# The first mixers' products added to h by VectorE from PSUM, in place of a staging tile and a GpSimd addition

## The chip, the core and the metric

The kernel runs on one core of a Trainium2 chip. The metric is the device time of one execution, in microseconds. The engines are named as the profile names them: PE is TensorE (matmuls), PEld its weight loads, DVE is VectorE, ACT is ScalarE, POOL is GpSimd, SP is SyncE, which issues the DMAs. SBUF is the on-chip memory, PSUM the accumulation memory that TensorE writes.

## The reference

One layer of a streaming encoder on 1024 frames of 1024 features, in float32:

```python
h = x
hn = rms_norm(h, norm_mix_g[i])
z_a, z_b, z_c, z_d = _split(hn @ w_in[i], [A_COLS, B_COLS, C_COLS, D_COLS])
o_a = gmlp_spatial_gating(z_a, ...)     # mixer 0
o_b = gated_deltanet(z_b, ...)          # mixer 1
o_c = rwkv7_time_mix(z_c, ...)          # mixer 2
o_d = conformer_conv(z_d, ...)          # mixer 3
h = h + jnp.concatenate([o_a, o_b, o_c, o_d], axis=-1) @ w_out[i]
hn = rms_norm(h, norm_ffn_g[i])
gate = causal_depthwise_conv(hn @ w_ffn_gate[i], ffn_conv_w[i])
h = h + (jax.nn.silu(gate) * (hn @ w_ffn_up[i])) @ w_ffn_down[i]
hn = rms_norm(h, norm_ple_g[i])
h = h + (p[i] @ w_ple_proj[i]) * jax.nn.sigmoid(hn @ w_ple_gate[i])
return rms_norm(h, final_norm_g)
```

Each mixer owns 256 of the 1024 columns. The line that matters here is the projection with `w_out`: it is a sum over the four mixers, so the kernel adds each mixer's part to h when that mixer's output is there.

## The kernel before

The frames are 8 tiles of 128 rows. Every matmul operand is split into a high part and a low part of a narrower type, and a product is three matmuls (`mm3`, L136): high by high, high by low, low by high.

The kernel has a first phase (input projection and the mixers' elementwise parts), a second phase (the recurrence of mixer 2, tile by tile), and then the feed-forward part and the last gate. At the end of the first phase VectorE inverts the lower triangular 32x32 blocks of mixer 2: `invert` is a chain of 31 steps, each with multiplications (L216) and subtractions (L220) on small SBUF operands, where each step needs the one before. In front of it a transposition makes its input (L1043, tile `rCs`), behind it two transpositions (L1147, L1149) give the tiles `rTc` and `Tn`, from which TensorE builds larger blocks (L1158, L1160). The tiles' recurrence can only start then.

`wout_early` gives TensorE work for that time: the parts of mixers 3 and 0, and then that of mixer 1. For each tile it loads the mixers' outputs (`oaf`), splits them (high part `osph` on ScalarE, L109; low part `ospl` on VectorE, L112) and multiplies them with the split weights (`wh`, `wl`), a half of 512 columns at a time: for mixers 3 and 0 a half is 12 matmuls into one of two PSUM buffers (the tag `psh`). In the first pass (`staged`, 8 tiles, 16 halves) ScalarE copies each half into the staging tile `stg` (L423), and GpSimd adds the tile to h (L425). In the other passes VectorE adds each half to h straight from PSUM (L427). The weights of mixers 1 and 2 are loaded and split (`wh` on ScalarE, `wl` on VectorE or GpSimd) into the buffers that the weights of mixers 3 and 0 leave. The staging tile shares its one buffer with `xn`, the normalised rows of a tile in `fnorm`.

A scheduler orders the instructions of each engine from their dependencies and priorities: the program's order is the priority, `tc.cur_priority` shifts whole parts back (`wout_early` by 100,000 and, for mixer 1, more), and `self.top()` puts what is made in it ahead of all else that is ready. An engine runs its instructions in the order so fixed, and each waits for the semaphores of what it needs.

Of the kernel before, what the change touches and what calls it, by code (L numbers as in the profile page):

```python
# [9 lines left out]
F32 = mybir.dt.float32  # L10
# [3 lines left out]
ALU = mybir.AluOpType  # L14
# [3 lines left out]
P = 128  # L18
S = 1024
D = 1024  # L20
# [77 lines left out]
class Net:  # L98
# [309 lines left out]
    def wout_tile(self, t, ofs, ws, staged=False, tag="osp", k="h"):  # L408

        nc = self.nc  # L410
        with self.top():
            os = [self.split(of, tag, [P, 2, P], 3 if tag == "osp" else 2, self.wo if tag == "osp" else self.p2) for of in ofs]
        for half in range(2):
            cs = slice(half * 512, half * 512 + 512)
            ps = self.mps(k)
            n = 2 * len(ofs)
            for j in range(n):
                (oh, ol), w = os[j // 2], ws[j // 2][j % 2]
                self.mm3(ps, oh[:, j % 2, :], ol[:, j % 2, :], w[0][:, cs], w[1][:, cs], j == 0, j == n - 1)
            if staged:  # L420
                if half == 0:
                    stg = self.wo.tile([P, D], F32, name="stg", tag="nxn", bufs=1)
                nc.scalar.copy(out=stg[:, cs], in_=ps)  # L423
                if half == 1:
                    nc.gpsimd.tensor_tensor(out=self.h[:, t, :], in0=stg, in1=self.h[:, t, :], op=ALU.add)  # L425
            else:
                nc.vector.tensor_tensor(out=self.h[:, t, cs], in0=ps, in1=self.h[:, t, cs], op=ALU.add)  # L427
            yield

# [1226 lines left out]
```

## Time and profile before

| | before |
|---|---|
| median of 3 runs | 1472.71 us (1472.57 to 1479.37) |
| the profiled execution | 1470.72 us |
| its span | 1468.9 us |
| TensorE busy | 1383.5 us (94%) |
| VectorE busy | 1038.8 us (71%) |
| ScalarE busy | 602.9 us (41%) |
| GpSimd busy | 467.2 us (32%) |
| mean granted clock of TensorE | 0.972 of 2.4 GHz |

A share of busy time is a mean over stages with different limits. A time in a row of the trace counts from the span's start. The time in brackets behind a row is what the engine stood idle before it, and behind the arrow is what ended that idle time.

### The profile page before, as it was taken

To read this page: it belongs to the slowest core of one execution; us is meant where nothing else is said; L and a number is where in the kernel's file an instruction comes from. 1 tells how busy PE (TensorE), PEld (TensorE's weight loads), DVE (VectorE), ACT (ScalarE), POOL (GpSimd) and SP (SyncE) were. 2 spreads that over 40 slices of the span, in tenths; PEclk is the share of its full clock that TensorE was granted. 3 is DMA by queue.
4 is the path that set the end of the run, shared out by engine and by line. 5 is a ranking of instruction groups with operands and counts; after the bars stand their busy time and mean duration, and the time that the engine had idled before them with its cause. 6 is when DMAs were issued, how large, how long until landed. Compare 5 with 4: busy or idle time off the path is not lost.

```text
span 1468.9 us, 21095 instructions
## 1 busy us (share of the span) xinstructions
PE 1383.5 (94%) x7864; PEld 1106.8 (75%) x7864; DVE 1038.8 (71%) x1773; ACT 602.9 (41%) x999; POOL 467.2 (32%) x432
## 2 busy tenths in 40 slices
PE   7998999799998889998799999999999999999997
PEld 6887877677766667776577888888888778877785
DVE  6599868776499677776487767776665695778543
ACT  7252363132642233336343333333333344445554
POOL 3304145262323341124421222222221454574000
PEclk9999999799999799999899999999999999999999
DMA  6111123132155333123533233322233993374132
GB/s 224 54 38 44 58 93 109 31 109 59 68 205 187 100 118 100 62 94 135 185 131 136 94 108 108 107 88 82 92 106 101 297 309 109 94 253 155 30 114 86
DMA packets 91734, 171.77 MB, mean 117 GB/s; under 512 B 12400, under 2 KB 41712, under 8 KB 91376
## 3 DMA queue, kind: packets, MB, share of 16 engines
q1 hardware_dynamic: 91344, 169.93, 34.8%
q8 instruction: 62, 1.02, 0.3%
q10 hardware_dynamic: 288, 0.49, 0.1%
q14 instruction: 40, 0.33, 0.1%
HBM read 120.85 MB, written 49.55 MB: 116 GB/s over the span
## 4 chain that ended last, share of the span: by engine, by line
PE 66%; DVE 18%; issue 5%; ACT 4%; POOL 3%; DMA 3%; SPq 0%; POOLq 0%; DVEq 0%; ACTq 0%
PE pf L136 40%; PE mps L136 13%; DVE cy L571 4%; DMA w<-in_wd 2%; DVE Xt L216 2%; DVE X L220 2%; PE mps L1082 1%; POOL wl L1227 1%; DVE wl L1227 1%; DVE w L1223 1%; PE mps L1178 1%; PE mps L879 1%; DVE by L195 1%; PE px L136 1%; PE mps L1160 1%
## 5 line engine op out<-in xcount | busy, mean ns | idle before, releaser
L136 PE MATMUL mps<-hT,wh 128*128 128x512 f32 (+1 forms) x736 | 233.8, 398 | 8.4 <-DVE by L195 3.8
L136 PEld LDWEIGHTS mps<-hT,wh 128*128 128x128 f32 x736 | 137.0, 192 | 39.7 <-issue 4.7
L136 PE MATMUL mps<-hT,wl 128*128 128x512 f32 (+1 forms) x368 | 145.5, 395 | 0.6 <-POOL wl L112 0.6
L1227 POOL TENSOR_TENSOR wl<-yr,wh 128x512 fp32r<-128x512 f32 x73 | 106.7, 1466 | 95.6 <-ACT wh L1226 82.9
L112 POOL TENSOR_TENSOR wl<-raw,wh 128x1024 fp32r<-128x1024 f32 x25 | 72.2, 2892 | 197.0 <-ACT wh L109 195.7
L136 PE MATMUL pf<-wl,wh 128*128 128x512 f32 x300 | 117.8, 392 | 3.9 <-DVE wl L1227 3.8
L136 PE MATMUL pf<-wh 128*128 128x512 f32 x300 | 117.1, 391 | 2.0 <-ACT wh L1226 2.0
L136 PE MATMUL pf<-wh,wl 128*128 128x512 f32 x300 | 117.0, 390 | 0.0
L1223 DVE TENSOR_TENSOR pf<-pf,u 128x512 f32<-128x512 f32 x88 | 61.0, 694 | 69.9 <-PE pf L136 69.8
L1226 ACT CAST fq<-s 128x512 fp32r<-128x512 f32 x88 | 53.5, 619 | 121.7 <-PE pf L136 96.5
L1227 POOL TENSOR_TENSOR fq<-raw,fq 128x512 fp32r<-128x512 f32 (+1 forms) x31 | 50.2, 1618 | 154.1 <-ACT fq L1226 154.1
L1227 DVE TENSOR_TENSOR wl<-w,wh 128x512 fp32r<-128x512 f32 x62 | 71.7, 1163 | 37.5 <-ACT wh L1226 37.2
L571 DVE SCALAR_TENSOR_TENSOR cy<-csg,prmt,cy 128x1023 f32<-128x1023 f32 (+29 forms) x60 | 83.0, 1408 | 7.1 <-ACT cy L568 6.6
L1227 POOL TENSOR_TENSOR wl<-raw,wh 128x1024 fp32r<-128x1024 f32 (+1 forms) x17 | 40.3, 2378 | 143.8 <-issue 116.6
L136 PEld LDWEIGHTS mps<-hT,wl 128*128 128x128 f32 x368 | 70.7, 192 | 16.5 <-issue 0.8
L1226 ACT CAST wh<-yr 128x512 fp32r<-128x512 f32 x73 | 45.1, 619 | 79.1 <-POOL wl L1227 49.4
L136 PEld LDWEIGHTS pf<-wl,wh 128*128 128x128 f32 x300 | 56.3, 188 | 18.1 <-DVE wl L1227 6.6
L1227 DVE TENSOR_TENSOR fq<-s,fq 128x512 fp32r<-128x512 f32 x66 | 45.5, 692 | 30.7 <-ACT fq L1226 30.7
L136 PEld LDWEIGHTS pf<-wh 128*128 128x128 f32 x300 | 56.3, 188 | 14.2 <-ACT wh L1226 2.5
L136 PE MATMUL pf<-xT2h,fq 128*128 128x512 f32 x176 | 60.4, 405 | 5.1 <-ACT fq L1226 5.1
L136 PEld LDWEIGHTS pf<-wh,wl 128*128 128x128 f32 x300 | 56.3, 188 | 11.3
L136 PE MATMUL pf<-xT4h,fq 128*128 128x512 f32 x176 | 59.1, 396 | 1.6 <-DVE pf L1223 1.6
(484 smaller groups left out, 3577.3 us busy)
## 6 DMA issues: line engine op xcount, KB each, us to landing
yr<-d_y SPq DMA_DIRECT2D x73, 256.0 KB, 3.0
w<-in_wd SPq DMA_DIRECT2D x55, 256.0 KB, 4.8
raw<-in_wg SPq DMA_DIRECT2D x24, 512.0 KB, 3.7
raw<-in_wu SPq DMA_DIRECT2D x24, 512.0 KB, 3.5
raw<-in_win SPq DMA_DIRECT2D x22, 512.0 KB, 3.7
d_y<-fy SPq DMA_DIRECT2D x11, 512.0 KB, 3.6
d_y<-ys SPq DMA_DIRECT2D x11, 512.0 KB, 3.4
d_y<-ys SPq DMA_DIRECT2D x22, 256.0 KB, 3.8
```

What stands on the lines that cost most here:

```text
L112: (eng or self.nc.vector).tensor_sub(out=lo, in0=raw, in1=hi.bitcast(F32))
L136: mm = lambda *a, **k: self.nc.tensor.matmul(*a, skip_group_check=more, **k)
L195: V.scalar_tensor_tensor(out=yh[:, j:], in0=ps[:, 0:512 - j], scalar=ws[j], in1=yh[:, j:], op0=ALU.mult, op1=ALU.add)
L216: nc.vector.tensor_tensor(out=t3[:, q], in0=A[:, j + 1 + q.start:j + 1 + q.stop, j:j + 1].broadcast_to([P, k, m]), in1=X[:, j:j + 1, 0:m]. ...
L220: nc.vector.tensor_tensor(out=X[:, rows, 0:m], in0=X[:, rows, 0:m], in1=t3[:, q], op=op)
L571: nc.vector.scalar_tensor_tensor(out=yc[:, sh:], in0=gl[:, 0:S - sh], scalar=self.prm("cfw", 2 * j + c), in1=yc[:, sh:], op0=ALU.mult, op1 ...
L879: nc.tensor.matmul(pS[:, pr * 64:pr * 64 + 64], x["E"][:, pr, c, :], S0[:, pr, :], start=True, stop=True)
L1082: nc.tensor.matmul(pa[:, pr, c], bk[rw, pr, c, :], cin[rw, 0:2, pr, cc[c]], start=True, stop=True)
L1160: nc.tensor.matmul(pq[c][r1, v], Q[r2, u], Tc[r2, u], start=True, stop=True)
L1223: eng.tensor_tensor(out=out, in0=a, in1=b, op=op)
L1226: self.nc.scalar.copy(out=hi, in_=raw)
L1227: eng.tensor_sub(out=lo, in0=raw, in1=hi.bitcast(F32))
```

## The change

In the staged pass, too, VectorE adds each half to h straight from PSUM, in the same form as in the other passes, and with the priority of `top()`. The two ScalarE copies and the GpSimd addition of each tile are gone, and with them the staging tile.

```diff
             for j in range(n):
                 (oh, ol), w = os[j // 2], ws[j // 2][j % 2]
                 self.mm3(ps, oh[:, j % 2, :], ol[:, j % 2, :], w[0][:, cs], w[1][:, cs], j == 0, j == n - 1)
-            if staged:
-                if half == 0:
-                    stg = self.wo.tile([P, D], F32, name="stg", tag="nxn", bufs=1)
-                nc.scalar.copy(out=stg[:, cs], in_=ps)
-                if half == 1:
-                    nc.gpsimd.tensor_tensor(out=self.h[:, t, :], in0=stg, in1=self.h[:, t, :], op=ALU.add)
-            else:
+            with self.top() if staged else nullcontext():
                 nc.vector.tensor_tensor(out=self.h[:, t, cs], in0=ps, in1=self.h[:, t, cs], op=ALU.add)
             yield
```

Lines behind the change have numbers that are lower by 6 in the changed kernel: L427 is L421 there, L1043 is L1037. The change also moves instructions on the engines. VectorE, in the middle of the inversion (`X` and `Xt` are its tiles, `ospl` a low part for TensorE), before:

```order
L216 TENSOR_TENSOR Xt<-rCs,X 128x108
L112 TENSOR_TENSOR ospl<-oaf,osph 128x256
L220 TENSOR_TENSOR X<-X,Xt 128x11x9
L220 TENSOR_TENSOR X<-X,Xt 128x12x9
L216 TENSOR_TENSOR Xt<-rCs,X 128x110 x2
L220 TENSOR_TENSOR X<-X,Xt 128x11x10 x2
L216 TENSOR_TENSOR Xt<-rCs,X 128x110
L216 TENSOR_TENSOR Xt<-rCs,X 128x121
L220 TENSOR_TENSOR X<-X,Xt 128x10x11
L112 TENSOR_TENSOR ospl<-oaf,osph 128x256
```

And the same place in the changed kernel:

```order
L216 TENSOR_TENSOR Xt<-rCs,X 128x108
L421 TENSOR_TENSOR h<-mps,h 128x512
L220 TENSOR_TENSOR X<-X,Xt 128x11x9
L220 TENSOR_TENSOR X<-X,Xt 128x12x9
L216 TENSOR_TENSOR Xt<-rCs,X 128x110 x2
L220 TENSOR_TENSOR X<-X,Xt 128x11x10
L112 TENSOR_TENSOR ospl<-oaf,osph 128x256
L220 TENSOR_TENSOR X<-X,Xt 128x11x10
L216 TENSOR_TENSOR Xt<-rCs,X 128x110
L216 TENSOR_TENSOR Xt<-rCs,X 128x121
L220 TENSOR_TENSOR X<-X,Xt 128x10x11
L421 TENSOR_TENSOR h<-mps,h 128x512
```

An addition stands where a low part stood, and the low part comes a few places later. Twelve of the sixteen additions stand between the transposition in front of the inversion and its last step: two in a row behind the second step, and then one about every ten rows.

GpSimd at the start of the second phase (`sbdT` is the operand built for a tile's recurrence, `rQ`, `rof` and `psp` other tiles of it and of filling work, `wl` a weight's low part), before:

```order
L1227 TENSOR_TENSOR psp<-pin,psp 128x256
L1101 TENSOR_SCALAR rQ<-rcin 128x256
L112 TENSOR_TENSOR wl<-raw,wh 128x1024
L1202 TENSOR_SCALAR sbdT_5047<-rTc 32x4x32 x4
L1204 TENSOR_SCALAR sbdT_5047<-rMo_3666 32x4x32 x2
L425 TENSOR_TENSOR h<-stg,h 128x1024
L1139 TENSOR_TENSOR rof<-rof,rcg 128x256
L1101 TENSOR_SCALAR rQ<-rcin 128x256
L112 TENSOR_TENSOR wl<-raw,wh 128x1024 x2
L1139 TENSOR_TENSOR rof<-rof,rcg 128x256 x2
```

And in the changed kernel, from the second tile's `rQ` on:

```order
L1095 TENSOR_SCALAR rQ<-rcin 128x256
L112 TENSOR_TENSOR wl<-raw,wh 128x1024
L1196 TENSOR_SCALAR sbdT_5031<-rTc 32x4x32 x4
L1198 TENSOR_SCALAR sbdT_5031<-rMo_3665 32x4x32 x2
L1095 TENSOR_SCALAR rQ<-rcin 128x256
L1221 TENSOR_TENSOR psp<-pin,psp 128x256
L112 TENSOR_TENSOR wl<-raw,wh 128x1024
L1196 TENSOR_SCALAR sbdT_5032<-rTc 32x4x32 x4
L1198 TENSOR_SCALAR sbdT_5032<-rMo_3665 32x4x32 x2
L1221 TENSOR_TENSOR psp<-pin,psp 128x256
L1095 TENSOR_SCALAR rQ<-rcin 128x256
L112 TENSOR_TENSOR wl<-raw,wh 128x1024
```

The three conversions of the weights of mixers 1 and 2 on GpSimd stand one in each of three tiles, the first two ahead of where the first stood. On ScalarE their high parts move with them. On TensorE 161 of the 192 matmuls of the staged pass stand in front of the first L1158, where 156 stood.

## Rows read from the trace of the kernel before

**Rows 1.** By stretches: us, busy us (instructions) by engine, PEclk, DMA share, GB/s.

```profile
445.00:470.00 25.00, 21.07 (x83) 16.57 (x83) 23.84 (x81) 6.63 (x15) 8.15 (x5) 0.93 0.48 165
...
485.00:505.00 20.00, 16.00 (x274) 12.75 (x275) 11.24 (x19) 4.06 (x8) 3.92 (x6) 0.50 0.17 48
570.00:600.00 30.00, 29.33 (x261) 22.74 (x260) 23.04 (x59) 11.97 (x28) 4.63 (x14) 1.00 0.21 71
```

**Rows 2.** PE in order of time: start us, us, instruction [idle before <-releaser].

```profile
456.74 0.50 PE L136 MATMUL mps<-wh,ospl 128*128 128x512 f32 x1 [3.72 <-DVE ospl L112]
...
458.12 0.63 PE L136 MATMUL mps<-wl,osph 128*128 128x512 f32 x1
458.55 0.63 PE L136 MATMUL mps<-wh,ospl 128*128 128x512 f32 x1
...
486.24 0.80 PE L136 MATMUL mps<-wh,ospl 128*128 128x512 f32 x1 [4.19 <-DVE ospl L112]
```

**Rows 3.** The staging tile's instructions: ns min/median/max, first and last start.

```profile
L423 ACT COPY stg<-mps x16: 578/586/593, 444.7 to 536.4; 128x512 f32<-128x512 f32 x16
L425 POOL TENSOR_TENSOR h<-stg,h x8: 2337/2376/2671, 446.2 to 539.8; 128x1024 f32<-128x1024 f32 x8
```

**Rows 4.** DVE in order of time, inside the inversion.

```profile
446.89 2.01 DVE L112 TENSOR_TENSOR ospl<-oaf,osph 128x256 fp32r<-128x256 f32 x1
...
451.87 2.54 DVE L216 TENSOR_TENSOR Xt<-rCs,X 128x56 f32<-128x56 f32 x2
454.33 0.33 DVE L220 TENSOR_TENSOR X<-X,Xt 128x56 f32<-128x56 f32 x2
...
456.27 0.42 DVE L112 TENSOR_TENSOR ospl<-oaf,osph 128x256 fp32r<-128x256 f32 x1
...
463.25 2.41 DVE L112 TENSOR_TENSOR ospl<-oaf,osph 128x256 fp32r<-128x256 f32 x1 [0.38 <-ACT osph L109]
...
469.38 2.41 DVE L216 TENSOR_TENSOR Xt<-rCs,X 128x126 f32<-128x126 f32 x1
...
472.04 0.28 DVE L216 TENSOR_TENSOR Xt<-rCs,X 128x126 f32<-128x126 f32 x1
...
476.10 2.47 DVE L220 TENSOR_TENSOR X<-X,Xt 128x110 f32<-128x110 f32 x1
...
483.57 2.28 DVE L216 TENSOR_TENSOR Xt<-rCs,X 128x60 f32<-128x60 f32 x1
```

**Rows 5.** POOL in order of time: two of the eight additions.

```profile
451.85 2.36 POOL L425 TENSOR_TENSOR h<-stg,h 128x1024 f32<-128x1024 f32 x1 [3.23 <-ACT stg L423]
...
539.78 2.36 POOL L425 TENSOR_TENSOR h<-stg,h 128x1024 f32<-128x1024 f32 x1
```

**Rows 6.** Groups of instructions: the addition from PSUM; busy us, mean ns | idle before.

```profile
L427 DVE TENSOR_TENSOR h<-mps,h 128x512 f32<-128x512 f32 x32 | 21.9, 687 | 7.8 <-PE mps L136 7.5
```

**Rows 7.** In order of time, 539 to 547 us: DVE, POOL and PE.

```profile
539.44 2.79 DVE L882 COPY sbdS<-rS 64x128 f32<-64x128 f32 x2
...
542.28 0.54 PE L896 MATMUL mps<-sbdS,rQ 128*64 128x128 f32 x5 [0.73 <-DVE sbdS L882]
...
544.26 0.73 PE L136 MATMUL mps<-wh,osch 128*128 128x512 f32 x2 [1.22 <-ACT wh L109]
544.29 4.78 POOL L112 TENSOR_TENSOR wl<-raw,wh 128x1024 fp32r<-128x1024 f32 x2 [0.86 <-ACT wh L109]
...
545.18 0.41 DVE L898 TENSOR_TENSOR oloc<-mps,oloc 128x256 f32<-128x256 f32 x1
...
546.66 2.50 DVE L882 COPY sbdS<-rS 64x128 f32<-64x128 f32 x2
...
546.73 0.79 PE L136 MATMUL mps<-wl,osch 128*128 128x512 f32 x1 [0.58 <-POOL wl L112]
```

**Rows 8.** L136 alone by stretches: us, PE busy (x), PEld busy (x), PEclk, DMA share, GB/s.

```profile
461.42:474.90 13.48, 13.48 (x60) 10.90 (x58) 1.00 0.64 210
485.00:505.00 20.00, 8.70 (x18) 5.48 (x19) 0.50 0.17 48
```

## The prediction

> **What bounds the kernel now.** I read the view by stretches first, then VectorE's instructions in order of time, then TensorE's, then the tile that the change removes. The changed products run while VectorE inverts the 32x32 blocks of the last mixer (L216 multiplies, L220 subtracts, each step needing the one before). In 445 to 470 us VectorE is busy 23.84 us of 25, TensorE 21.07 [rows 1]: VectorE sets the end here and TensorE waits for it, for instance 3.72 us and 4.19 us for VectorE's low part of a mixer output [rows 2]. In 485 to 505 us TensorE holds a granted clock of 0.50, the 1.2 GHz level; from 570 us it is busy 29.33 us of 30 at 1.00 [rows 1]. So time won in the inversion arrives at the end, and behind it TensorE is the bound: there its idle time counts, not VectorE's.
>
> **What is removed.** Sixteen ScalarE copies of 586 ns and eight GpSimd additions of 2,376 ns [rows 3]. ScalarE waits for TensorE in this stretch, so its copies are worth nothing by themselves. The GpSimd additions are worth much, through VectorE: while one runs, a VectorE instruction that reads SBUF takes as long as the addition does. The six that fall in the inversion have each one such row [rows 4]. Against the nearest undisturbed row of the same kind:
>
> - L112 at 446.89: 2.01 - 0.42 = 1.59 us
> - L216 at 451.87 (a pair): 2.54 - 0.33 = 2.21
> - L112 at 463.25: 2.41 - 0.42 = 1.99
> - L216 at 469.38: 2.41 - 0.28 = 2.13
> - L220 at 476.10: 2.47 - 0.28 = 2.19
> - L216 at 483.57: 2.28 - 0.28 = 2.00
>
> The GpSimd rows at 451.85 and 539.78, 2.36 us each, show the pattern [rows 5]. Sum: 12.11 us off VectorE's chain.
>
> **What is added.** Sixteen VectorE additions of 128x512 from PSUM. The kernel has 32 of that form: 687 ns each [rows 6]. The order of the changed kernel puts twelve of them between the first transposition and the end of the inversion: 12 x 0.687 = 8.24 us on the same chain. Net for the inversion: -12.11 + 8.24 = -3.87 us. The four later ones stand where VectorE is busy 11.24 us of 20 [rows 1]; I cost them at nothing, and at 4 x 0.687 = 2.7 us if that gap is gone. A GpSimd instruction beside them should not stretch them: the addition from PSUM at 545.18 took 0.41 us under a GpSimd pair that ran from 544.29 to 549.07, when the SBUF copy at 546.66 took 2.50 [rows 7].
>
> **The added wait.** Each addition waits for its half product: 12 matmuls of 512 columns. Behind it on VectorE stand the rest of the inversion and the low parts that TensorE needs next. At clock 1.00 a matmul starts every 13.48 / 58 = 0.23 us (58 weight loads in that stretch [rows 8]), so a half takes 2.8 us; at the lower clock one starts every 0.43 us (458.12 to 458.55 [rows 2]), 5.2 us a half. VectorE's pace: from 451.87 to the end of the row at 483.57 are 34.0 us [rows 4]; less the five stalls in it (10.5) and with ten additions (6.9) that is 30.4 us for ten halves, against 27.9 us that TensorE needs at full clock. Slack: 2.5 us. There are two PSUM buffers, and the first two additions come only after two steps of the inversion, some 5 us after the ScalarE copies of before (first at 444.7 [rows 3]). TensorE pauses that long. After its pause of 3.72 us the clock was at the lower level from 458.12 [rows 2] to 461.42, where a stretch at 1.00 begins [rows 8]: 3.3 / 0.43 = 8 matmuls, 0.2 us lost on each, 1.6 us. That fits into 2.5. I take 0 for the wait; the bounds are 0 and, if the clock stays low twice as long and some low parts come late, +2.4 us.
>
> The page "TensorE: Matmul & The Clock Gate" of the Trainium skill (section "A second HAM failure mode: psum-queue depth-cycling") speaks against this change: a kernel that cycles through PSUM buffers can let TensorE idle briefly so often between groups that its clock swings, and throughput is lost. What that would do here is the third rival below; the trace agrees in one place (the 8 matmuls), and not in the 13.48 us that follow at 1.00.
>
> **What moves.** The output weights of the other two mixers reuse the buffers of these two, and their conversion stands a tile earlier on GpSimd and ScalarE, as the orders show. Before, TensorE waited at 544.26 for such a weight (1.22 us), at 546.73 for its low part (0.58), and at 542.28 for a VectorE copy of 2.79 us that the GpSimd addition at 539.78 stretched (0.73) [rows 5, 7]. Those 2.53 us are TensorE's own idle time; I take all of them off. Bounds: 0 (the converted weights, 4.78 us for two on GpSimd [rows 7], stretch other VectorE rows where they stand now) and -2.53. SyncE's queue changes with this: the loads of the weights go ahead of two of mixer outputs; they wait for GpSimd's conversions, which are earlier too, so I cost that at nothing.
>
> **TensorE's low clock at 485 to 505.** It has 18 matmuls of 512 columns [rows 8], at 0.43 us instead of 0.23. The changed order has five more before the inversion ends, so the pause ahead of it is shorter. A full clock would give 18 x 0.2 = 3.6 us. A pause stays, since TensorE still has to wait for the last transposition, so I take 0; bounds 0 and -3.6.
>
> **Sum.** -3.87 - 2.53 = -6.4 us. The profiled execution took 1470.72 us, so 1464.3 on its scale; the median of the runs shown, 1472.71, lies 2.0 us above it: 1466.3 us.
>
> **Rivals.**
>
> 1. The gain is larger: the clock does not fall at 485. For it: TensorE's 4.19 us wait ahead of that stretch ends earlier, with more work before it. Against: another pause remains, and small matmuls follow. 1466.3 - 3.6 = 1462.7 us.
> 2. No change: the additions wait after all. VectorE and TensorE now hand each other a low part one way and a PSUM buffer the other, with a slack of a quarter of a microsecond per half. If each of the ten additions loses 0.4 us, the 3.87 us are gone; with the weights' gain gone too, 1472.7 us. For it: the thin slack. Against: VectorE's low parts stand right behind the additions, early enough by the same pace.
> 3. Slower: in the inversion TensorE stays at the lower clock. Ten halves then take 120 x 0.43 = 51.6 us in place of 30.4, and VectorE stands behind each: +21.2 - 3.9 = +17.3, 1490 us. It decides when more than 2.5 / 0.2 = 12 of the 120 matmuls run at the lower level; another 3.87 / 0.2 = 19 eat the inversion's gain, and with the weights' 2.53 us and the 7.4 us of the bound below it takes some 80 to be slower beyond it. Against: the trace came back to 1.00 after 8.
>
> **How the numbers follow.** Chances: forecast 0.50, first rival 0.20, second 0.22, third 0.08. A change under 0.5% (7.4 us, so 1465.3 and 1480.1) can hardly be told from none in this kernel. Faster than that: the first rival and the better part of the forecast (about two fifths of it), 0.41; slower: the third rival and a little more, 0.09; between: 0.50. Range: down 3.6 us for the clock and up to 3.7 us that the two stretched VectorE copies of 2.79 and 2.50 us [rows 7] may have held back beyond the waits listed; up 2.5 + 2.4 us for the weights and the wait, and 2.7 for the four later additions: 1459 to 1474. The third rival is outside.
>
> **What would show it.** Right: no row of L216, L220 or L112 near 2.4 us in the inversion; twelve additions of about 0.69 us in it with under 2.5 us of waits for TensorE; its last transposition about 4 us earlier; no GpSimd wait at 540 to 547. Wrong: a granted clock near 0.5 between 450 and 480 (third rival), many waits of VectorE for TensorE at the additions (second), or the same time gained up to 505 and lost again before 660.

## The result and the profile after

| | before | changed |
|---|---|---|
| median | 1473.85 us (1472.57 to 1479.37, 4 runs) | 1457.08 us (1454.70 to 1461.12, 4 runs) |
| the profiled execution | 1470.72 us, span 1468.9 | 1459.43 us, span 1457.6 |
| mean granted clock | 0.972 | 0.977 |
| ScalarE busy | 602.9 us | 594.5 us |
| GpSimd busy | 467.2 us | 448.6 us |

The ratio of the times is 0.9884 (95% interval 0.9858 to 0.9909): 1.2% faster. The forecast was 1466.3 us in a range from 1459 to 1474, so the time lies below the range and the gain of 16.8 us is 2.6 times the 6.4 us of the sum. Executions over 1.5% above the fastest of their kernel, at a lower clock, are in no median, range or ratio here (one of four_psum, two of stage_dve).

The stretches that answer to [rows 1], of the changed kernel (us, busy us of PE, PEld, DVE, ACT and POOL, granted clock, DMA share, GB/s):

```profile
445.00:470.00 25.00, 20.08 (x77) 16.14 (x77) 23.78 (x97) 2.44 (x6) 0.00 (x0) 0.86 0.58 207
485.00:505.00 20.00, 18.10 (x324) 14.11 (x325) 11.74 (x24) 5.42 (x11) 5.82 (x13) 0.86 0.50 150
570.00:600.00 30.00, 29.80 (x253) 23.20 (x251) 23.17 (x72) 10.06 (x25) 3.36 (x9) 1.00 0.22 71
```

GpSimd does nothing in the first stretch, VectorE is as full as before, and between 485 and 505 us the clock is mostly up where it was at 0.50 (it falls to 0.50 at 499.4 us, for 10.2 us; in the second profile of this kernel it does not).

VectorE's rows in and behind the inversion, in order of time:

```profile
445.69 1.24 DVE L1037 STREAM_TRANSPOSE rCs<-rCd 128x1024 f32<-128x1024 f32 x1
...
449.18 1.28 DVE L421 TENSOR_TENSOR h<-mps,h 128x512 f32<-128x512 f32 x2
450.38 0.31 DVE L216 TENSOR_TENSOR Xt<-rCs,X 128x42 f32<-128x42 f32 x2
...
455.33 0.69 DVE L421 TENSOR_TENSOR h<-mps,h 128x512 f32<-128x512 f32 x1 [0.33 <-PE mps L136]
455.94 0.43 DVE L220 TENSOR_TENSOR X<-X,Xt 128x99 f32<-128x99 f32 x2
...
469.34 0.68 DVE L421 TENSOR_TENSOR h<-mps,h 128x512 f32<-128x512 f32 x1
469.94 0.41 DVE L112 TENSOR_TENSOR ospl<-oaf,osph 128x256 fp32r<-128x256 f32 x1
...
481.73 2.08 DVE L1141 STREAM_TRANSPOSE rTc<-X 128x1024 f32<-128x1024 f32 x1
483.66 1.96 DVE L1143 STREAM_TRANSPOSE Tn<-X 128x1024 f32<-128x1024 f32 x1
```

No row of L216, L220 or L112 in the inversion is near 2.4 us any more, against the six of [rows 4]. The twelve additions wait once, 0.33 us. An addition takes 0.68 to 0.69 us, but what follows it starts 0.60 us later (469.34 to 469.94; 455.33 to 455.94 is 0.61), since the rows overlap.

TensorE in the changed kernel: the rows in front of which it idles longest, and the block products (L1152, L1154):

```profile
449.92 0.79 PE L136 MATMUL mps<-wh,osph 128*128 128x512 f32 x1 [6.06 <-DVE h L421]
...
485.76 1.20 PE L1152 MATMUL mps<-Tn,rMo 32*32 32x32 f32 x64 [1.43 <-DVE Tn L1143]
...
487.79 1.19 PE L1154 MATMUL mps<-rTc,Q 32*32 32x32 f32 x61
...
532.06 0.33 PE L1128 MATMUL mps<-ident,oloc 128*128 128x128 f32 x1 [1.58 <-DVE oloc L469]
536.31 0.50 PE L136 MATMUL mps<-wh,osch 128*128 128x512 f32 x1 [1.06 <-ACT osch L109]
544.70 0.50 PE L136 MATMUL mps<-wh,osph 128*128 128x512 f32 x1 [0.78 <-DVE h L421]
```

And the same block products before (L1158, L1160), which the prediction did not look at:

```profile
491.08 1.92 PE L1158 MATMUL mps<-Tn,rMo 32*32 32x32 f32 x64 [2.76 <-DVE Tn L1149]
...
494.51 1.89 PE L1160 MATMUL mps<-rTc,Q 32*32 32x32 f32 x60
```

Before, they begin behind a pause of 2.76 us (and one of 4.19 five microseconds earlier [rows 2]) and a group of 64 takes 1.9 us, at the lower clock. Now they begin 5.3 us earlier, behind 1.43 us, and a group takes 1.2. The waits of TensorE at 540 to 547 us [rows 7] are gone, but others of 1.58, 1.06 and 0.78 us stand near there.

To see the whole account, one stretch is taken in each profile: from 440 us to the first product of the last gate (`px`). Behind it every kernel here needs 795 to 800 us. The columns are those of the first fence; `again` and `before2` are second profiles of the changed kernel and of the kernel before (below). First the kernel before, then before2, the changed kernel, again:

```profile
440.00:672.82 232.82, 211.13 (x1701) 162.41 (x1699) 172.48 (x481) 78.48 (x176) 63.33 (x86) 0.93 0.34 112
```

```profile
440.00:680.86 240.86, 221.12 (x1698) 170.70 (x1697) 170.14 (x482) 78.87 (x177) 63.00 (x86) 0.89 0.33 108
```

```profile
440.00:661.14 221.14, 204.14 (x1700) 158.96 (x1699) 166.16 (x497) 70.09 (x160) 43.75 (x78) 0.96 0.36 118
```

```profile
440.00:656.66 216.66, 200.47 (x1700) 156.09 (x1699) 166.00 (x497) 70.11 (x160) 43.89 (x78) 0.97 0.37 121
```

TensorE's idle time is the length less its busy time. What the clock costs is, as an estimate, the length times one less the clock; the two digits of the clock leave an error of about 1.2 us. The rest is the work at full clock:

| profile | length | idle | clock | rest |
|---|---|---|---|---|
| before | 232.8 | 21.7 | 16.3 | 194.8 |
| before2 | 240.9 | 19.7 | 26.5 | 194.7 |
| changed | 221.1 | 17.0 | 8.8 | 195.3 |
| again | 216.7 | 16.2 | 6.5 | 194.0 |

The work is the same in all four, as it must be. The first profiles differ by 11.7 us, 4.7 of idle time and 7.5 of clock; again differs from before by 16.2 us, about the gain in the medians: 5.5 of idle time and 9.8 of clock. And two executions of one kernel can differ by the clock: before2 idles 2.0 us less than before, and its stretch is 8.0 us longer.

### The profile page after: what moved, and what is told of

It reads as the page before. It is cut to its first block, busy times and chain, and to the rows that moved or that the text cites. A ratio compares the mean times of both kernels' runs of the same rounds, so it can differ in the third digit from the quotient of the medians.

```text
span 1457.6 us, 21083 instructions
## 1 busy us (share of the span) xinstructions
PE 1377.5 (95%) x7864; PEld 1102.8 (76%) x7864; DVE 1034.1 (71%) x1789; ACT 594.5 (41%) x983; POOL 448.6 (31%) x424
## 4 chain that ended last, share of the span: by engine, by line
PE 44%; DVE 4%; issue 3%; POOL 3%; DMA 2%; ACT 2%; SPq 0%; POOLq 0%; DVEq 0%; ACTq 0%
PE pf L136 40%; POOL wl L1221 2%; DMA w<-in_wd 1%; PE mps L136 1%; PE px L136 1%; DVE w L1217 1%; DVE wl L1221 1%; DVE t L1217 0%; ACT wh L1220 0%; DMA d_f<-fo 0%; DVE s L1217 0%; PE pf L1563 0%; PE mps L1076 0%; DMA early<-in_wd 0%; POOL t L1217 0%
## 5 line engine op out<-in xcount | busy, mean ns | idle before, releaser
L136 PE MATMUL mps<-hT,wh 128*128 128x512 f32 (+1 forms) x736 | 234.1, 398 | 8.4 <-DVE by L195 3.8
L136 PEld LDWEIGHTS mps<-hT,wh 128*128 128x128 f32 x736 | 137.1, 192 | 40.0 <-issue 4.6
L136 PE MATMUL mps<-hT,wl 128*128 128x512 f32 (+1 forms) x368 | 145.6, 396 | 0.3 <-POOL wl L112 0.3
L112 POOL TENSOR_TENSOR wl<-raw,wh 128x1024 fp32r<-128x1024 f32 x25 | 72.2, 2886 | 206.8 <-ACT wh L109 205.5
L136 PE MATMUL pf<-wl,wh 128*128 128x512 f32 x300 | 118.3, 394 | 3.4 <-DVE wl L1221 3.4
L136 PE MATMUL pf<-wh 128*128 128x512 f32 x300 | 117.4, 392 | 2.0 <-ACT wh L1220 2.0
L136 PE MATMUL pf<-wh,wl 128*128 128x512 f32 x300 | 117.5, 392 | 0.0
L136 PEld LDWEIGHTS mps<-hT,wl 128*128 128x128 f32 x368 | 70.6, 192 | 16.4 <-issue 0.8
L136 PEld LDWEIGHTS pf<-wl,wh 128*128 128x128 f32 x300 | 56.7, 189 | 17.9 <-DVE wl L1221 6.3
L136 PEld LDWEIGHTS pf<-wh 128*128 128x128 f32 x300 | 56.5, 189 | 14.2 <-ACT wh L1220 2.4
L136 PEld LDWEIGHTS pf<-wh,wl 128*128 128x128 f32 x300 | 56.8, 189 | 11.6
L136 PE MATMUL pf<-xT2h,fq 128*128 128x512 f32 x176 | 60.2, 403 | 5.4 <-ACT fq L1220 5.4
L136 PE MATMUL pf<-xT4h,fq 128*128 128x512 f32 x176 | 59.0, 396 | 1.5 <-DVE pf L1217 1.5
```

The costliest lines, as they stand in the source:

```text
L112: (eng or self.nc.vector).tensor_sub(out=lo, in0=raw, in1=hi.bitcast(F32))
L136: mm = lambda *a, **k: self.nc.tensor.matmul(*a, skip_group_check=more, **k)
```

## The experiments

All ratios are to the kernel before on the same chip, run beside the kernel in question (medians 1472.70, 1474.10 and 1472.10 us in the three sets of runs).

**again** is the changed kernel without any edit.

> The changed kernel as it is, for a second profile and a tighter ratio: the first gave 0.9884 of the time before (0.9858 to 0.9909), but its own profiled execution was only 11.3 us shorter than the profiled one of before. Theory (the gain is made up to the end of the inversion and of the block products: about 4 us less idle time of TensorE and about 6 us less time at the lower clock): ratio 0.987 to 0.992, the granted clock 1.00 while the block products run, those ending 8 to 10 us earlier than in the profile of before. Rival (most of what goes beyond the forecast is chance between runs, since the clock's dips fall elsewhere in each): ratio 0.992 to 0.996.

Measured: 1456.32 us (1454.98 to 1459.39), ratio 0.988 (0.9854 to 0.9906). The block products end at 492.3 us, 9.4 us earlier than before, with a granted clock of 1.00. The gain is not chance, and the theory's number held. Its row for 485 to 505 us:

```profile
485.00:505.00 20.00, 18.70 (x345) 14.47 (x347) 13.02 (x25) 7.42 (x15) 6.58 (x14) 1.00 0.58 169
```

**pool_back** puts GpSimd's load back and nothing else (the scratch tile is read by nobody, and VectorE's instructions keep their order):

```diff
             with self.top() if staged else nullcontext():
                 nc.vector.tensor_tensor(out=self.h[:, t, cs], in0=ps, in1=self.h[:, t, cs], op=ALU.add)
+            if staged and half == 1:
+                stg = self.wo.tile([P, D], F32, name="stg", tag="nxn", bufs=1)
+                nc.gpsimd.tensor_tensor(out=stg, in0=self.h[:, t, :], in1=self.h[:, t, :], op=ALU.add)
             yield
```

> The changed kernel with eight GpSimd additions of 128x1024 in SBUF put back, one per tile, written to a scratch tile that nothing reads; VectorE's additions from PSUM stay and the order of TensorE and VectorE is the same. Theory (each GpSimd addition stretches one VectorE row that reads SBUF to about 2.4 us, and the later end of the inversion lets TensorE's clock fall): six rows of VectorE near 2.4 us again, the inversion 10 to 12 us longer, a stretch at granted clock 0.50 over the block products, 1467 to 1476 us, so no better than before. Rival (GpSimd's load doesn't matter, the gain is that of the staging copies and the order): 1455 to 1460 us.

Measured: 1476.58 us (1473.67 to 1479.53), ratio 1.001 (0.9987 to 1.0033): 20.3 us slower than again, just above the theory's range, and the whole gain is gone. GpSimd's rows, and then three of the six VectorE rows beside them:

```profile
474.81 1.95 POOL L424 TENSOR_TENSOR stg<-h 128x1024 f32<-128x1024 f32 x1 [3.52 <-DVE h L421]
482.07 1.95 POOL L424 TENSOR_TENSOR stg<-h 128x1024 f32<-128x1024 f32 x1 [5.32 <-DVE h L421]
489.37 1.95 POOL L424 TENSOR_TENSOR stg<-h 128x1024 f32<-128x1024 f32 x1 [5.35 <-issue]
```

```profile
474.93 1.97 DVE L216 TENSOR_TENSOR Xt<-rCs,X 128x120 f32<-128x120 f32 x1
482.19 2.10 DVE L216 TENSOR_TENSOR Xt<-rCs,X 128x75 f32<-128x75 f32 x2
489.49 1.88 DVE L220 TENSOR_TENSOR X<-X,Xt 128x31 f32<-128x31 f32 x1
```

Each VectorE row ends within 0.3 us of the GpSimd row. The page "SBUF — State Buffer" of the Trainium skill (section "Who interferes with whom") says this in a rule: a VectorE instruction with two inputs in SBUF and a GpSimd instruction that reads SBUF contend for a shared pair of ports, which is an exclusive lock, and a VectorE instruction with at most one SBUF input does not contend, outside the modes in which it uses both ports. The rows agree with the first half. For the second, [rows 7] had an addition from PSUM of 0.41 us in the middle of a GpSimd pair; but the copy of `sbdS` there, with one SBUF input, took 2.50 us, and no run here shows in which mode it ran.

The inversion ends at 491.4 us, 9.7 later than in again, TensorE pauses 4.47 us ahead of the block products, and the clock is at 0.50 behind it. The stretch from 440 us to `px`:

```profile
440.00:676.07 236.07, 210.22 (x1703) 163.40 (x1701) 178.62 (x499) 70.68 (x161) 61.40 (x87) 0.93 0.34 111
```

It is 19.4 us longer than in again: 25.9 us of idle time in place of 16.2, and 16.5 us for the clock in place of 6.5 by the same estimate. So GpSimd's load alone takes back both halves of the gain.

**no_add** is the kernel before with GpSimd's addition cut to 8 columns; it leaves nearly all of these products out of h.

```diff
-                    nc.gpsimd.tensor_tensor(out=self.h[:, t, :], in0=stg, in1=self.h[:, t, :], op=ALU.add)
+                    nc.gpsimd.tensor_tensor(out=self.h[:, t, 0:8], in0=stg[:, 0:8], in1=self.h[:, t, 0:8], op=ALU.add)
```

> The kernel before with GpSimd's additions of the staged pass cut from 1024 to 8 columns, so that nearly all of these products are left out of h; the copies, the order on TensorE and the rest stay. Theory (the additions cost through VectorE's stretched rows): the inversion is 10 to 12 us shorter, TensorE's waits of 3.72 and 4.19 us for low parts are gone, and the time is 10 to 16 us shorter, 1457 to 1464 us. Rival (the stretched rows are hidden, TensorE's matmuls set the end of this stage): within 4 us of before.

Measured: 1460.82 us (1456.34 to 1469.80), ratio 0.9927 (0.9896 to 0.9959). The inversion ends at 475.9 us, 10.9 earlier than before; the six stalls were estimated at 12.1, and VectorE waits in it for 2.25 us in place of 0.54. But this kernel, with hardly any addition, is no faster than the changed one with sixteen. TensorE runs out of work, and the block products come behind a pause and at the lower clock:

```profile
480.25 1.92 PE L1158 MATMUL mps<-Tn,rMo 32*32 32x32 f32 x64 [3.30 <-DVE Tn L1149]
```

Its stretch from 440 us to `px`, in the columns of the stretches above:

```profile
440.00:667.39 227.39, 213.74 (x1699) 165.01 (x1699) 159.02 (x481) 78.60 (x176) 46.54 (x86) 0.92 0.35 115
```

It idles 13.7 us there, the least of all, and pays 18.2 us for the clock.

**back_early and back_late** put one of the eight GpSimd additions back (`if staged and half == 1 and t == 1`, or `t == 5`).

> The changed kernel with one GpSimd addition of 128x1024 (to a scratch tile) put back, behind the second tile's additions, about a quarter into the inversion; the order of TensorE and VectorE is that of the changed kernel. Theory (a stretched row costs its own 2 us, and beside that TensorE loses a much larger amount only where its pause ahead of the block products grows past about 3 us, as 4.19, 3.30 and 4.47 us did in the profiles of before, of the kernel without the additions and of the one with all eight put back, against 1.43 in the changed kernel): one row near 2.4 us, the pause ahead of the block products still under 2 us, the clock at 1.00 there, 1457 to 1460 us against 1456.3. Rival (every stretched row costs the same, a sixth of the 20 us that all eight cost): 1459 to 1460.5 us, and the same as the late one within 1.5 us.

> The same with the one GpSimd addition behind the sixth tile's additions, at the end of the inversion. Theory: one row near 2.4 us, TensorE's pause ahead of the block products grows by 2 us to 3 to 4 us, its granted clock is 0.50 for some 15 us behind it, and the time is 4 to 8 us longer than with the early one: 1462 to 1467 us. Rival (every stretched row costs the same): 1459 to 1460.5 us, as the early one.

Measured: 1461.07 us (1459.55 to 1462.98), ratio 0.9907 (0.9878 to 0.9936), and 1462.32 us (1461.17 to 1464.37), ratio 0.9917 (0.9887 to 0.9946). The late one's time and its clock (0.50 from 488 us for 14 us, behind a pause of 2.99 us) fit the theory, but the theory wanted it 4 to 8 us slower than the early one, and it is slower by 1.3 us, with ranges that overlap. The early one does not fit, since I had taken its stall to be spent before the block products. The rival was right that the two cost the same within 1.5 us; its size, 3.3 us for each, is missed by both: 4.8 and 6.0 us. One stretched row is already followed by a drop of the clock over the block products. The early one's TensorE and its whole stretch:

```profile
486.27 1.20 PE L1155 MATMUL mps<-Tn,rMo 32*32 32x32 f32 x64 [2.53 <-DVE Tn L1146]
```

```profile
440.00:660.94 220.94, 205.22 (x1700) 160.23 (x1698) 166.22 (x496) 69.64 (x160) 46.12 (x79) 0.95 0.36 118
```

The inversion's last transposition ends 0.56 us later than in again (486.12 for 485.56), and TensorE's idle time in the stretch is 15.7 us for 16.2. What grew is the clock's part: 11.0 us for 6.5. So the clock accounts for the whole 4.3 us by which this stretch is longer than again's; it fell at 488 us, behind a pause of 2.53 us where again has 1.44. Against the first profile of the changed kernel the stretch is no longer at all (220.9 for 221.1 us), since the clock fell in that one too, at 499.4 us; over all executions the table in the next section has the same split. This is the nearest that the runs come to the clock's price by itself.

**stage_dve** keeps ScalarE's copies and the staging tile and changes only the engine that adds and its priority: `nc.vector` under `self.top()` in place of `nc.gpsimd`, 128x1024.

> The kernel before with its staging tile and ScalarE's copies, but the addition of each tile made by VectorE (128x1024, both operands in SBUF, ahead of all else that is ready) in place of GpSimd. Theory (GpSimd's load on VectorE's rows is what the change took away; where VectorE's operand lies doesn't matter): no row near 2.4 us in the inversion, about 1.2 us for each addition, TensorE's pause of 5 to 6 us ahead of the inversion is not there since ScalarE frees the PSUM buffers, 1450 to 1460 us. Rival (reading PSUM directly is what helps): 1465 us or more.

Measured: 1458.10 us, ratio 0.990 (0.987 to 0.993), with the widest scatter of all: 1452.09 to 1473.73. The additions take 1.22 us each, no row in the inversion is stretched, and it ends when again's does (481.7). So GpSimd was what cost; that the operand lies in PSUM is not needed for it. The scatter has a place in the profile too:

```profile
502.83 0.80 PE L136 MATMUL mps<-wh,osph 128*128 128x512 f32 x1 [4.49 <-DVE h L428]
```

At the start of this pause, at 498.5 us, the clock fell, and the profiled execution (1468.39 us) stayed at the lower level for 47.8 us.

**four_psum** and **first_staged** go after TensorE's 6.06 us at 449.92. In four_psum the halves take turns over two more PSUM buffers (`self.mps("hb"[t % 2] if staged else k)`); in first_staged ScalarE copies the first tile's halves and VectorE adds that tile in one instruction from SBUF.

> The changed kernel with four PSUM buffers for the staged halves in place of two (every other tile takes those of another tag, idle in this stage). Its profile shows TensorE idle for 6.06 us before the inversion starts, until the first addition frees a buffer, and about 12 matmuls at the lower clock after it. Theory (TensorE's lost time in this stage is the gain that is left): no pause over 1 us there, the staged products done before the block products start, 5 to 9 us faster than the changed kernel, 1448 to 1452 us. Rival (VectorE's chain sets the end here, and TensorE's pause is only moved): 1454 to 1459 us.

> The changed kernel, but the two halves of the first tile are copied by ScalarE to a staging tile and VectorE adds that in one instruction; the other tiles go straight from PSUM. Theory (TensorE's pause of 5 to 6 us ahead of the inversion and the low clock behind it are the loss that is left): the pause under 2 us, clock 1.00 from 447 to 480 us, two more additions and three more low parts in the inversion (2 us longer), in all 2 to 7 us faster than the changed kernel: 1449 to 1455 us. Rival (as with four PSUM buffers, VectorE's longer chain takes it all): 1456 to 1462 us.

Measured: 1460.80 us (1455.54 to 1464.70), ratio 0.9907 (0.9886 to 0.9929), and 1465.83 us (1461.64 to 1471.10), ratio 0.9952 (0.9931 to 0.9973). The theory fell in both, and both medians lie above the rival's range as well. The pause is gone (1.39 and 1.95 us), but TensorE's faster products put more additions and low parts into VectorE's chain, and the inversion ends at 489.4 and 486.9 us in place of 481.6. In four_psum a GpSimd conversion of the next weights, pulled into the inversion, stretches a VectorE row again (L112 on a weight, 3.38 us at 483.37, for 1.22). Taking away TensorE's pause ahead of the inversion won nothing in either; a run without the pause and with VectorE's chain unaltered was not made.

**no_top and top_last** take the raised priority from all sixteen additions, or from all but the last four (`if staged and t >= 6`).

> The changed kernel without the raised priority: VectorE's additions stand where the program's order puts them, 155 in place of 161 staged matmuls come before the block products. Theory (the priority matters little, since an addition is ready about when VectorE comes to it, but a later low part lengthens TensorE's pause ahead of the block products): 1455 to 1464 us, with the clock low over the block products if that pause is above 3 us. Rival (without the priority TensorE waits for PSUM buffers at each half): TensorE idle over 15 us in the inversion and 1468 us or more.

> The changed kernel with the raised priority only on the additions of the last two tiles (four of the sixteen, behind the inversion); without any raised priority it was 1470.75 us although its inversion ended 1.6 us earlier, at 480.0. Theory (the priority matters behind the inversion, where an addition that is late holds up TensorE and the weights that follow): 1456 to 1461 us. Rival (the priority matters in the inversion, where six staged matmuls fewer fit in): 1466 to 1472 us.

Measured: 1470.75 us (1465.04 to 1472.43), ratio 0.9966 (0.9945 to 0.9986), and 1460.92 us (1459.70 to 1464.23), ratio 0.9924 (0.9911 to 0.9937). My expectation for no_top fell by 7 us, and its rival's reason as well: the inversion ends at 480.0 us. The expectation for top_last held. The loss is behind the inversion. Three late additions stand in a row there, with TensorE waiting for the first, and the weights of the other mixers are split 24 us later (VectorE's low part at 526.20 for 502.43):

```profile
550.19 0.50 PE L136 MATMUL mps<-wh,osph 128*128 128x512 f32 x1 [2.40 <-DVE h L421]
```

In both profiles the clock also falls over the block products (to 0.50 from 485.7 to 499.3 us in no_top, from 486.7 to 500.3 in top_last), where again's stays at 1.00. By the ratios the changed kernel (again) gains 1.20%, without any raised priority 0.34%, and with it on the last four alone 0.76%. So most of the gain hangs on the priority as well as on GpSimd, and about half of that on the four additions behind the inversion, which the prediction priced at nothing; that price was right only because they have it.

**weights_dve** gives VectorE the last three low parts of weights that GpSimd makes (`(nc.vector, nc.vector)` in the two loads).

> The changed kernel with the low parts of the output weights of the other two mixers made by VectorE in place of GpSimd (three of 128x1024 move). The second profile of the changed kernel has three VectorE rows of 2.4 us or less behind the inversion, at 504.5, 525.2 and 543.4, beside those conversions. Theory (the lock costs there too): those rows gone, three of 1.23 us more on VectorE, TensorE idle 1 to 3 us less from 500 to 550 us, 1451 to 1455 us. Rival (VectorE has slack there, the rows are hidden): 1455 to 1459 us.

Measured: 1456.19 us (1450.55 to 1463.20), ratio 0.9893 (0.987 to 0.9915): as the changed kernel. The two VectorE rows that these conversions stretched in again (2.37 us at 504.46, and a group of four at 524.99 that took 3.01) are gone, three of 1.23 us are new, and no gain can be measured. That fits the rival, that the stretched rows are hidden where VectorE has slack; with intervals of about 3 us to either side it doesn't prove it.

**before2** is the kernel before without any edit.

> The kernel before as it is, for a second profile. Between 440 us and the first product of the last gate, its first profile has 21.7 us of TensorE idle and 27.5 us busy at the lower clock; the changed kernel's two profiles 17.0 and 16.7, and 16.2 and 8.2. Theory (the pause ahead of the block products brings the clock down in each execution of before): granted clock 0.50 for 10 to 20 us from about 485 us again, 24 us or more busy at the lower clock in all, six rows of VectorE near 2.4 us. Rival (the first profile of before was an unlucky one): under 15 us at the lower clock.

Measured: 1472.11 us (1466.85 to 1481.51), ratio 1.0009. Behind 2.80 us of waiting for the last transposition the clock is at 0.50 from 489 to 506 us. In the inversion five rows are stretched, not six; the sixth GpSimd addition ran from 484.99 to 487.40 us beside the first transposition, which took 2.08 us, as in again without one (2.09). Its lower clock is not at the block products alone: in the stretch to `px` it spends some 37 us more at 0.50, in five other places.

None of these kernels is measurably faster than the changed one.

## Why the prediction was wrong, step by step

**The inversion: right in kind, over 1 us short.** From the start of the first transposition to the end of the last row the inversion took 41.0 us (445.73 to 486.77) and takes 36.0 (445.69 to 481.70), in again 35.5. That is 5.0 to 5.5 us where the sum had 3.87. The stalls were priced well: by the spacing of starts the rows of L216, L220 and L112 in it take 26.3 us in place of 38.8. That any VectorE instruction that reads SBUF is held was too wide (before2's transposition was not), but it changed no term. The additions were priced at their duration, 0.687 us; by their spacing of 0.60 they cost 12 x 0.60 = 7.2 us, and 12.11 - 7.2 = 4.9.

**The added wait: right.** 0.33 us in all. The pause at 449.92 and the 12 matmuls at the lower clock behind it fit into the slack.

**The waits of the second phase: wrong, harmlessly.** The 2.53 us were not won. From the end of the block products to `px` TensorE idled 9.85 us before and 9.29 and 9.50 after: three waits went and others came. To take all of a list of waits as gain, without asking what stands behind each, was the error; the two errors nearly cancel, so that idle time fell by 4.7 to 5.5 us against the 6.4 of the sum.

**TensorE's clock at 485 to 505: the step that failed.** I took 0 with a bound of -3.6 us, and the clock gave about 7.5 and 9.8 us in the two profiles, counted to `px`; in 485 to 505 us itself it went from 0.50 to 0.86 and to 1.00. Two things were wrong. The bound counted the 18 matmuls of 512 columns [rows 8] and left out the 256 others: TensorE was busy 16.00 us in that stretch [rows 1], all of it at half the full clock, so a full clock would have given up to 8 us. The row that said so was quoted. And the choice of 0 rested on "a pause stays". One does, but of 1.43 us in place of 4.19 and 2.76, and the clock stayed up over the block products. So the first rival happened, with the mechanism that it named, at a price more than twice its own.

One profile of a kernel can be a lucky or unlucky one, so here is the same estimate over the means of all executions (span times one less the mean granted clock; back_early belongs to another set of runs, whose kernel before has a rest of 1428.7 and 44.6 us for the clock):

| kernel, executions | mean span | clock | rest |
|---|---|---|---|
| before, 24 | 1472.6 | 43.8 | 1428.8 |
| again, 6 | 1454.8 | 32.3 | 1422.5 |
| pool_back, 12 | 1474.7 | 45.4 | 1429.4 |
| no_add, 7 | 1461.5 | 41.2 | 1420.3 |
| back_early, 6 | 1459.1 | 36.2 | 1422.8 |

Each mean is uncertain by about 1 us (no_add's clock by 2). The rest fell by 6.3 us, which is the sum's 6.4 (by luck, since two errors cancel in it), and the clock gave 11.5 us that the sum had at nothing. pool_back loses both again, and back_early is longer than again by the clock.

How firmly is the pause shown as the cause? The pause ahead of the block products was 2.53 to 4.47 us in seven profiles (before, before2, pool_back, no_add, back_early, back_late, first_staged), and the block products ran at the lower clock in all of them, in back_early and back_late in all but the first group. It was 1.12 to 1.84 us in seven others; in five of them the clock stayed at 1.00 through the block products (changed, again, weights_dve, stage_dve, four_psum), and in two (no_top 1.54, top_last 1.51) it fell 1.2 to 1.4 us behind the pause. (In four_psum another pause, of 3.10 us ahead of a weight, was followed by 3.4 us at the lower clock before the block products began.) In before it had fallen at 485.1 us already, within the wait of 4.19 us in front of that pause, and in changed and weights_dve it fell at 499.4 and 499.5 us, behind the block products and behind no pause over 0.7 us. So it was low behind every long pause, behind a short one sometimes, and it also fell without one. The small block products alone do not bring it down: again ran them at 1.00. A kernel with the pause filled and nothing else altered was not tried; that GpSimd's load costs the clock is shown by pool_back, that it does so through the pause is an association over fourteen profiles and not a separate proof.

The third rival, beside which the page "TensorE: Matmul & The Clock Gate" of the Trainium skill stood (section "A second HAM failure mode: psum-queue depth-cycling": brief idle times between groups let the clock swing), did not occur: with its two PSUM buffers cycling, TensorE ran the inversion's products at 1.00 from 455 us on, in both profiles of the changed kernel.

## What to carry to other kernels

Price a stretch at a low clock by all that TensorE does in it, and treat a pause that the change shortens as a price of its own: here the clock gave more than the waiting that was saved. A GpSimd addition in SBUF of 2.4 us cost 1.6 to 2.2 us each on a VectorE chain of SBUF operands that has no slack, and taking such rows away where there is slack won nothing measurable. Time an engine's instruction in a chain by the spacing of starts, and ask of a priority what it does for the last few instructions, not only for the many.

## What the runs showed of the hardware

- The same program on the same chip scatters by 1%, and its time goes with the clock: the executions of before2 reach from 1466.85 us at a mean granted clock of 0.973 to 1481.51 at 0.962 and 0.965.
- A shorter chain is not a shorter kernel: no_add has the shortest inversion and the least idle time, and its profiled stretch from 440 us to `px` was 6.3 us longer than the changed kernel's, 227.4 for 221.1, since the clock took 18.2 us of it in place of 8.8.
